# Adaptive max pooling: the loads of the first group walk each partition's run from its high end to its low end

## Chip, cores and metric

The kernel runs on one core of a Trainium2 chip. The metric is the device time of one execution in microseconds (us). Before the prediction, three runs of the kernel before gave 334.97 us (median; 334.90 to 335.02). The profile is one further execution, with a span of 333.2 us.

## The reference

```python
x = np.random.randn(32, 256, 4096).astype(np.float32)   # batch, channels, length
output_size = 256

for i in range(output_size):
    start = int(i * length / output_size)
    end = int((i + 1) * length / output_size)
    result[:, :, i] = np.max(x[:, :, start:end], axis=-1)
```

The length divides evenly, so each output is the maximum of 16 neighbouring values (64 B). 134.2 MB are read, 8.4 MB are written, and each value is used once.

## The kernel before

All outputs are one long list. It is split into group A (128 x 9340 outputs) and group B (128 x 7044), and inside a group each of the 128 partitions (the rows of the on-chip memory, SBUF) owns a contiguous run. The distance between the starts of two neighbouring partitions' runs is called the pitch: 597,760 B in group A, 450,816 B in group B. A load brings up to 1024 outputs' worth of every partition's run, 64 KiB per partition and 8.39 MB in all. VectorE, the compute engine that takes the maxima, reduces it in two pieces, and the outputs collect in the tile `kept`, which is stored at the end. In the code, `W` is the 16 values of one output.

```python
    CHUNK = 1024
    GAP = 152
    FIRST = 128
    LOADS_A, LOADS_B = 9, 6

    LESS = 4
    group_a = [FIRST] + [CHUNK] * (LOADS_A - 1) + [CHUNK - LESS]
    last = total - sum(group_a) - LOADS_B * CHUNK
    group_b = [CHUNK] * LOADS_B + [last]
    # ... cut ...
    for g, loads in enumerate((group_a, group_b)):
        xg, og = group(sum(loads))      # one contiguous run per partition
        a = 0
        for n in loads:
            xn = xg[:, a * W : (a + n) * W]
            dst = kept[:, base + a : base + a + n] if n != last else None
            if n == FIRST:
                # ... cut: the small first load and its reduction ...
            else:
                low = n_loads % 2 * (CHUNK + GAP)
                moved = n_loads // 2 % 2
                at = low + moved * GAP
                nc.sync.dma_start(out=ring[:, at * W : (at + n) * W], in_=xn)
                if n != last:
                    cut = CHUNK - GAP if moved else GAP
                    parts = [(0, cut), (cut, n)]
                    for u, v in parts if moved else parts[::-1]:
                        pooled(dst[:, u:v], at + u, v - u)
                # ... cut: the last load, reduced in place ...
                n_loads += 1
            a += n
        full = a - last if g else a
        stores.append((og[:, 0:full], kept[:, base : base + full]))
        base += full
```

The ring holds two loads and a gap. A new load goes over the larger part of the load before last, so it is issued as soon as that part's reduction (872 outputs) has ended, and does not wait for the smaller part (152). The two large stores are issued after the last load.

## Time and profile before

| | before |
|---|---|
| time, median of 3 | 334.97 us |
| VectorE busy | 276.5 us (83%) |
| 16 DMA engines busy with the queue of the loads and the two large stores | 98.8% |
| rate over the span | 428 GB/s |
| one full load, landing to landing | 19.3 to 19.4 us |
| VectorE's work for one full load | 17.28 us |

The lines behind these figures, and how they are read, are in the prediction. A landing is the moment when a load has arrived, read from the start of the reduction that waited for it; a round is the time from one landing to the next.

### The profile page before, as it was taken

How to read it: one execution, taken by the hardware profiler on the slowest of the kernel's cores; microseconds unless marked ns; L12 is line 12 of the kernel's file. 1: busy time of each engine (PE TensorE's matmuls, PEld its weight loads, DVE VectorE, ACT ScalarE, POOL GpSimd, SP SyncE). 2: the span in 40 equal slices, each digit the busy share in tenths (PEclk: the TensorE clock that was granted, in tenths of full speed). 3: DMA queues.
4: the chain of work that ended last, by engine and by line, in shares of the span. 5: the costliest groups of instructions: out<-in, count | busy, mean ns of one | idle time of the engine just before them, and what ended most of it. 6: DMA issues, size and time to landing. Idle time of an engine off the chain costs nothing.

```text
span 333.2 us, 113 instructions
## 1 busy us (share of the span) xinstructions
DVE 276.5 (83%) x32; POOL 0.2 (0%) x4
## 2 busy tenths in 40 slices
DVE  2009979797997979799797979979797998979993
POOL 0000000000000000000000000000000000000000
DMA  9898989899898989899898989899898989899987
GB/s 378 378 504 378 504 378 504 378 409 472 378 504 378 504 378 504 378 417 464 376 502 377 504 378 496 386 425 456 378 504 378 504 378 504 378 458 443 393 386 339
DMA packets 2880, 142.61 MB, mean 428 GB/s; under 512 B 320, under 2 KB 320, under 8 KB 448
## 3 DMA queue, kind: packets, MB, share of 16 engines
q1 hardware_dynamic: 2736, 142.15, 98.8%
q10 hardware_dynamic: 144, 0.46, 0.3%
HBM read 134.22 MB, written 8.39 MB: 428 GB/s over the span
## 4 chain that ended last, share of the span: by engine, by line
DMA 57%; DVE 36%; DVEq 5%; issue 0%; SPq 0%
DMA ring<-in_x_dram 57%; DVE kept L56 36%; DVEq L145 5%; SPq L85 0%
## 5 line engine op out<-in xcount | busy, mean ns | idle before, releaser
L56 DVE TENSOR_REDUCE kept<-ring 128x152 f32<-128x2432 f32 (+3 forms) x31 | 261.4, 8473 | 51.6 <-DMA ring<-in_x_dram 51.6
L56 DVE TENSOR_REDUCE ring<-ring 128x900 f32<-128x14400 f32 x1 | 15.1, 15141 | 0.0
L131 POOL MEMSET const-bfloat16-1.0<- 128x1 bf16 x1 | 0.1, 102 | 0.0
L131 POOL MEMSET const-uint8-127<- 128x1 uint8 x1 | 0.1, 101 | 0.0
L131 POOL MEMSET const-float32-0.0<- 128x1 f32 x1 | 0.1, 99 | 0.2 <-issue 0.2
L131 POOL MEMSET const-float32-1.0<- 128x1 f32 x1 | 0.1, 98 | 0.0
## 6 DMA issues: line engine op xcount, KB each, us to landing
ring<-in_x_dram SPq DMA_DIRECT2D x1, 8160.0 KB, 24.0
ring<-in_x_dram SPq DMA_DIRECT2D x1, 7200.0 KB, 21.6
out_dram<-kept SPq DMA_DIRECT2D x1, 4670.0 KB, 32.4
out_dram<-kept SPq DMA_DIRECT2D x1, 3072.0 KB, 18.1
ring<-in_x_dram SPq DMA_DIRECT2D x1, 1024.0 KB, 4.6
out_dram<-ring ACTq DMA_DIRECT2D x1, 450.0 KB, 4.2
ring<-in_x_dram SPq DMA_DIRECT2D x14, 24.0
```

The source lines that it names most:

```text
L56: nc.vector.reduce_max(out=dst, in_=ring[:, at * W : (at + n) * W].rearrange("p (n w) -> p n w", w=W), axis=mybir.AxisListType.X,)
L131: nc = _bacc.Bacc("TRN2", target_bir_lowering=False, num_devices=1)
L145: with _tile.TileContext(nc) as tc:
```

## The change

The ten loads of group A keep their sizes and their order in time, but the first one now takes the top of each partition's run, and the following ones walk down. The place in `kept` moves along, so the result and the stores stay. The intent was to learn whether the direction of the walk through memory is worth something.

```diff
--- before.py
+++ after.py
@@ -76,8 +76,10 @@
     base = 0
     for g, loads in enumerate((group_a, group_b)):
         xg, og = group(sum(loads))
-        a = 0
+        a = sum(loads) if g == 0 else 0
         for n in loads:
+            if g == 0:
+                a -= n
             xn = xg[:, a * W : (a + n) * W]
             dst = kept[:, base + a : base + a + n] if n != last else None
             if n == FIRST:
@@ -102,8 +104,9 @@
                     last_kept = ring[:, end - n : end]
                     pooled(last_kept, at, n)
                 n_loads += 1
-            a += n
-        full = a - last if g else a
+            if g:
+                a += n
+        full = a - last if g else sum(loads)
         stores.append((og[:, 0:full], kept[:, base : base + full]))
         base += full
     assert taken == total
```

## The prediction

> **What bounds the kernel now.** I read the page first, from the top: busy shares, the row of the DMA engines, and the bytes moved.
>
> ```profile
> span 333.2 us, 113 instructions
> ...
> DVE 276.5 (83%) x32; POOL 0.2 (0%) x4
> ...
> DMA  9898989899898989899898989899898989899987
> ...
> HBM read 134.22 MB, written 8.39 MB: 428 GB/s over the span
> ```
>
> One compute engine works at all, for 83% of the span; the 16 DMA engines are nearly full in every slice (the 8s and 9s come from the way a 64 KiB packet is booked to a slice). The mean of 428 GB/s is over everything, start and tail included. So the DMA engines are the suspect, and the next view must say whether they ever pause. That is the stretches view, cut at the landings of the loads; its last two columns are the DMA share and GB/s. Group A is the loads up to about 179 us, group B those from there to 312.8, and the last stretch is the stores.
>
> ```profile
> 0.00:24.73 24.73, 2.29 (x1) 0.20 (x4) 1.00 1.00 424
> 24.73:44.10 19.37, 17.28 (x2) 0.00 (x0) 1.00 1.00 433
> ...
> 121.50:140.90 19.40, 17.28 (x2) 0.00 (x0) 1.00 1.00 432
> 140.90:160.30 19.40, 17.28 (x2) 0.00 (x0) 1.00 1.00 432
> ...
> 218.30:237.70 19.40, 17.28 (x3) 0.00 (x0) 1.00 1.00 432
> ...
> 312.80:333.20 20.40, 15.29 (x2) 0.00 (x0) 1.00 0.89 382
> ```
>
> Every load of 8.39 MB takes 19.3 to 19.4 us, with the DMA share at 1.00, and VectorE needs only 17.28 us of that. The reader is to see two things: the DMA engines set the pace, not VectorE, and group A (24.73 to 160.30) and group B (218.30 to 237.70) run at the same rate.
>
> The third view is the chain that ended last. It looks as if VectorE and loads alternate:
>
> ```profile
> 24.75 14.70 DVE kept L56
> 39.45 0.02 issue
> 39.47 24.06 DMA ring<-in_x_dram
> 63.52 0.02 issue
> 63.55 14.70 DVE kept L56
> ```
>
> This is not a proof that VectorE is on the path. A load is issued at 39.47, when the 14.70 us reduction has freed its room, and lands at 63.52; but the load before it landed only at 44.13 (where the next reduction starts in the timeline). For 44.13 - 39.47 = 4.66 us the new load waits behind the previous one in a full queue. The remaining 19.4 us are its own transfer. So VectorE has about 4.7 us of room in each round before the queue would run dry, less the gap between last byte and semaphore. The view of waits agrees: VectorE waits for loads, and nobody else waits on the compute side.
>
> ```profile
> DVE kept L56 <- DMA ring<-in_x_dram: 51.6, 16, 17.1
> ```
>
> Of these 51.6 us, 17.1 is the first full load and 5.4 the small one before it; the other 14 waits are about 2.1 us each, which is 19.35 - 17.28.
>
> Last, the packet records of the trace: each partition's row is one packet of 65,536 bytes, its median time is 2.418 to 2.422 us in every full load, in group A and group B, and the worst of all is 2.64 us. 16 engines x 65,536 B / 2.418 us = 433.6 GB/s. A time that constant looks like a fixed limit of the engine or its port and not like memory that answers now well and now badly.
>
> **What the Trainium skill says.** "DMA: Bandwidth & Descriptors", section "Where 436 GB/s comes from", gives the ceiling on the SBUF side as 16 ports x 256 bits x 850 MHz = 435.2 GB/s. The trace agrees: 432 to 435 in the full stretches. "HBM Reference", section "Specifications (TRN2)", gives about 716 GB/s to the pair of cores that share a memory, and says that a core streaming alone is bounded by its 16 DMA engines. With one core running, the trace has 433, so by these pages some 280 GB/s of memory bandwidth are idle, an estimate from the two. The DMA page, section "Latency and other measured facts", reports that rows whose pitch is a large power of two (512 KiB and up) cost half the rate or more, and that padding by 4 KiB cures it. That is the one thing by which addresses alone could matter here. The same page, section "How a descriptor splits into AXI transactions", says that a run that does not start at a multiple of 256 B fetches bytes that it does not use. The trace of before shows neither loss.
>
> **The change part by part.** Only the source address and the place in `kept` move, and only for the ten loads of group A.
>
> - Removed or added: no instruction, no byte, no semaphore. The list of sizes is walked in the same order (128, then eight of 1024, then 1020), so the first load is still 1.0 MB, the ring slots alternate as before (they depend on the count of loads, not on the offset), and the reductions have the same 32 shapes. VectorE: 276.5 us before and after, difference 0.
> - Moved, source: one partition's run of group A is 9340 x 64 B = 597,760 B. Before, the loads start at 0, 8,192, 73,728 and so on upwards inside it; after, at 589,568, 524,032, ..., 65,280 and 0. The pitch between partitions stays 597,760 B = 2335 x 256, no power of two. The new starts are multiples of 256 as well (524,032 = 2047 x 256; 65,280 = 255 x 256). Modulo 4096, partition p of a full load started at -256p before and starts at -256(p + 1) now: the same set of 16 residues, shifted by one partition. Inside one row the bytes still go upwards, and the distance between the 16 rows in flight is unchanged. Cost: ten loads at an unchanged 433 GB/s, 0.
> - Moved, target: `kept` of group A is filled from the top. Start addresses of the reductions' outputs in it were multiples of 32 B and are now multiples of 16 B (1020 x 4 = 4080). VectorE reads 16 values for each one it writes, so I expect nothing; were a reduction a few hundred ns longer, it would vanish in the 2.1 us of idle time and the 4.7 us of queue.
> - The stores: same bytes, same shape, same order. All of group A's outputs are there when its last reduction ends near 197 us, and its store is issued at 291.5 us, after the last load. Cost 0.
>
> Sum: 0, so 334.97 stays, rounded to 335.0.
>
> **The rivals.** First, a memory rate that depends on the addresses: running backwards breaks a neighbourhood that the memory used. Before, the next load starts where the last ended, in the same partition's run, but some 19 us later, and after 8.4 MB of other addresses. For it: this kernel's odd size of 1020 suggests that somebody tuned the pitch. Against it: pitch and stagger are what that tunes, and they stay; and the kernel before holds a natural trial, since group B has another pitch (450,816 B, residues going up instead of down) and the same 432 GB/s. What it would make: 2% is 6.7 us, over about 175 us of group A's transfers a rate 3.8% lower, 417 instead of 433 GB/s. Five per cent lower would give about 344 us.
>
> Second, a new wait: the tracker of dependences could see the descending writes into `kept`, or the moved slice of 1020, as a hazard and hold a load or the first store. For it: the code that orders things looks at addresses. Against it: within a group no two reductions write the same part of `kept` and none reads it; the ring, where the real hazards are, is addressed exactly as before. If the first store were held until the last reduction, it would cost up to its own transfer, 4.78 MB at 433 = 11 us, of which part lies beside that reduction; some 340 us.
>
> Third, a gain. The loads could run nearer to the skill's 435.2 GB/s: at most 0.4% of 175 us, 0.7 us. The start cannot gain, since the first load is as small as before and VectorE then waits for the second one anyway. Over 2% faster has no room in a stretch that is full at 433.
>
> Fourth, the transfer that is hidden anyway: VectorE's changed alignment, above. Hidden in both directions.
>
> **Range and chances.** The three runs of before span 0.12 us, and the steps above sum to 0. The range must hold a different chip or run, and tenths of a microsecond from slow packets (the first full loads of before had a few of 2.5 to 2.6 us, about 0.1 us per load when spread over 16 engines). I take 334.4 to 335.8, a little longer upwards, as losing rate is possible and gaining it hardly is. Within 2%: 0.96. Slower by over 2%: 0.03, the first two rivals. Faster by over 2%: 0.01.
>
> **What would show it.** Right: the stretches between landings in group A stay at 19.3 to 19.4 us and 432 to 435 GB/s, packets stay near 2.42 us, VectorE's sum stays at 276.5 us, the first store is still issued near 291.5 us, and the chain has the same 36 pieces. Wrong by the first rival: group A's stretches over 20 us with DMA share 1.00 and fewer GB/s, group B's unchanged. Wrong by the second: a pause in the DMA row, or the first store issued after 310 us. Wrong on the target's alignment: a mean of the 872-wide reduction other than 14.69 us, with no effect on the span below some 16.7 us (14.69 + 2.07).

## The result and the profile after

The changed kernel took 334.92 us (median of 6 runs, 334.86 to 335.00), the kernel before 334.97 us (6 runs, 334.83 to 335.13). The ratio is 0.9999, with a 95% interval of 0.9986 to 1.0012. A ratio here is the mean time of one kernel's runs over that of the other's of the same rounds, so it is not quite the ratio of the medians. Executions over 1.5% slower than the fastest of the same kernel are left out of the means.

Set side by side, the two programs have the same instructions in the same order on every engine; only line numbers differ. The page of the kernel after:

```profile
span 333.1 us, 113 instructions
...
DVE 276.5 (83%) x32; POOL 0.2 (0%) x4
...
HBM read 134.22 MB, written 8.39 MB: 428 GB/s over the span
```

The span is 0.1 us shorter, and the other lines shown are as before. The stretches of the kernel after, over the same windows (length, VectorE busy, two columns without use here, DMA share, GB/s):

```profile
24.73:44.10 19.37, 17.28 (x2) 0.00 (x0) 1.00 1.00 433
121.50:140.90 19.40, 17.30 (x3) 0.00 (x0) 1.00 1.00 432
140.90:160.30 19.40, 17.32 (x3) 0.00 (x0) 1.00 1.00 432
...
218.30:237.70 19.40, 17.33 (x3) 0.00 (x0) 1.00 1.00 432
...
312.80:333.20 20.40, 15.16 (x2) 0.00 (x0) 1.00 0.89 382
```

The first three of these are group A, which now goes downwards; the rates are those of before to the last digit. The 17.30 to 17.33 in place of 17.28 come from where the windows cut: the reductions start some hundredths earlier. The groups of reductions by shape (busy us, mean ns of one, idle before), in the kernel before:

```profile
L56 DVE TENSOR_REDUCE kept<-ring 128x872 f32<-128x13952 f32 x14 | 205.6, 14686 | 44.3 <-DMA ring<-in_x_dram 44.3
L56 DVE TENSOR_REDUCE kept<-ring 128x152 f32<-128x2432 f32 x15 | 40.1, 2676 | 0.0
```

And after:

```profile
L56 DVE TENSOR_REDUCE kept<-ring 128x872 f32<-128x13952 f32 x14 | 205.6, 14686 | 44.1 <-DMA ring<-in_x_dram 44.1
L56 DVE TENSOR_REDUCE kept<-ring 128x152 f32<-128x2432 f32 x15 | 40.1, 2676 | 0.0
```

The means are the same to the nanosecond. So the moved target cost nothing either, and the null is not a sum of two effects that cancel: source and target are each unchanged. The wait of VectorE after, as one line:

```profile
DVE kept L56 <- DMA ring<-in_x_dram: 51.5, 16, 17.1
```

It was 51.6 before. The packet records of the trace say the same for the memory side: 64 KiB packets took a mean of 2.421 us after and 2.422 us before, with 4 of 1792 over 2.5 us after and 18 before.

### The profile page after: what moved, and what is told of

The parts are those of the page before. It is cut to its first block, busy times and chain, and to the rows that moved or that the text cites. A ratio compares the mean times of both kernels' runs of the same rounds, so it can differ in the third digit from the quotient of the medians.

```text
span 333.1 us, 113 instructions
## 1 busy us (share of the span) xinstructions
DVE 276.5 (83%) x32; POOL 0.2 (0%) x4
## 4 chain that ended last, share of the span: by engine, by line
DMA 57%; DVE 36%; DVEq 5%; issue 0%; SPq 0%
DMA ring<-in_x_dram 57%; DVE kept L56 36%; DVEq L148 5%; SPq L87 0%
```

## Experiments

The theory was: the loads run at a limit (2.418 us for a 64 KiB packet on each of 16 engines) that lies in front of the memory, so that the order of the addresses is not seen; and VectorE lies beside the loads. The main rival was: the memory does care where the loads go, and upward and downward happen to suit it equally. A second rival took the chain of the profile literally, with VectorE on the path. All kernels give correct results but that of e1. Each group of runs has its own runs of the kernel before on the same chip (medians 334.86, 334.97 and 335.14 us).

### e1: read the same place nine times

```diff
-            xn = xg[:, a * W : (a + n) * W]
+            if g == 0 and n != FIRST:
+                xn = xg[:, FIRST * W : (FIRST + n) * W]
+            else:
+                xn = xg[:, a * W : (a + n) * W]
```

The results of group A are wrong.

> Nine full loads of group A all read the first full load's 8.39 MB again (outputs of group A wrong on purpose; every instruction and byte count as before). Theory (the engine and port limit of 2.418 us per 64 KiB packet sets the pace, the memory's order is not seen): 335.0 us within 0.3%, packets at 2.42 us. Rival (the memory's neighbourhood matters, and the forward and the backward walk happen to be equally good or bad): rereading the same 8.39 MB must move the rate of group A, by more than 1% of the span in one direction or the other.

Measured: 335.50 us (335.33 to 335.91), ratio 1.0018 (1.0003 to 1.0033). The median packet is still 2.418 us, but 31 of 1792 took over 2.5 us, against 18 in the trace of before. In the middle of group A, the rate goes down a little and comes back in group B (the stretches of e1):

```profile
121.81:141.41 19.60, 17.28 (x2) 0.00 (x0) 1.00 0.99 428
141.41:160.99 19.58, 17.28 (x3) 0.00 (x0) 1.00 0.99 428
219.25:238.60 19.35, 17.27 (x3) 0.00 (x0) 1.00 1.00 434
```

Inside the 0.3% of the theory and far from the rival's 1%. Reading one place again and again gains nothing, and costs about 0.6 us (by the interval, 0.1 to 1.1 us). Why it costs those was not looked into.

### e2: shuffle both groups

```diff
-        for n in loads:
+        order = (0, 6, 1, 8, 4, 7, 2, 5, 3, 9) if g == 0 else (4, 1, 5, 0, 3, 2, 6)
+        starts = [sum(loads[:i]) for i in range(len(loads))]
+        for i in order:
+            a, n = starts[i], loads[i]
...
-            a += n
+            a = sum(loads)
```

> The loads of both groups in a scrambled order, with no two neighbours in a row in either direction; result correct. Theory: 335.0 us within 0.3%, stretches of 19.3 to 19.4 us. Rival (memory likes any regular walk, forward or backward): slower than 2%, rates under 425 GB/s in both groups.

Measured: 334.84 us (334.77 to 335.17), ratio 0.9998 (0.9983 to 1.0013). One pair of neighbours slipped through: in group B, load 2 follows load 3. Group A has none. A regular walk is worth nothing that 0.5 us would show in this layout. One stretch of group A and one of group B of e2:

```profile
121.54:140.89 19.35, 17.28 (x2) 0.00 (x0) 1.00 1.00 434
218.22:237.57 19.35, 17.28 (x3) 0.00 (x0) 1.00 1.00 434
```

### e3 and e4: a layout in which addresses cost something

A test that finds nothing must show that it could have found something. Here each partition's run is its whole 1 MiB of the input, so that the 16 rows in flight lie multiples of 1,048,576 B apart, not of 597,760 or 450,816 B. Sizes and instructions are as before. The rows of the stores move too: they now lie 65,536 B apart in the output, not 37,360 or 28,176 B. e3 walks up; e4 has the change on top.

```diff
-        span = slice(taken * P, (taken + n) * P)
+        lo = taken
         taken += n
         return (
-            xw[span].rearrange("(p n) w -> p (n w)", p=P),
-            ow[span].rearrange("(p n) -> p n", p=P),
+            xw.rearrange("(p n) w -> p (n w)", p=P)[:, lo * W : taken * W],
+            ow.rearrange("(p n) -> p n", p=P)[:, lo:taken],
         )
```

> Positive control: before's order, but one partition's run is its whole 1 MiB, so the pitch of the rows in flight is 1,048,576 B and no longer 597,760 or 450,816 B; same instructions and bytes, correct result. If addresses can be felt at all in this kernel, here: by the Trainium skill's pitch figures for 512 KiB to 4 MiB I estimate loads at 200 to 350 GB/s, so 420 to 700 us. If it is 335 us too, the memory's addresses are not felt even in the worst layout that I know, and the theory is stronger than I stated it.

> The same 1 MiB pitch with the changed kernel's downward order of the first group. Theory: order is not seen even where the memory may be the limit, so the same as e3 within 1%. Rival (order matters once the memory is the bound, and it was hidden before only by the port limit): over 2% away from e3.

Measured: e3 353.53 us (352.78 to 355.84), ratio 1.0577 (1.0538 to 1.0616); e4 355.46 us (354.16 to 357.10), ratio 1.0614 (1.0578 to 1.0650). So addresses can be felt in this kernel, which is what the control was for. The stores have little part in it: of the 17.8 us by which the profiled span of e3 is longer (351.0 us for 333.2), 16.2 have come by the issue of the first large store (307.70 us for 291.50). My estimate of 420 to 700 us was far too high, and the fault is in how I read the page, in the prediction too. The Trainium skill ("DMA: Bandwidth & Descriptors", section "Latency and other measured facts") has 207 GB/s at a pitch of 512 KiB, 164 at 2 MiB and 103 at 4 MiB, where a padded pitch has 214. The loss is about half at 4 MiB; at 512 KiB it is 3%, and at 2 MiB 23%. The 5.5 to 5.8% by which the kernel got longer here at 1 MiB lie between these. The stretches of e3, cut at its landings:

```profile
28.61:51.59 22.98, 17.28 (x3) 0.00 (x0) 1.00 0.99 385
91.03:111.33 20.30, 17.28 (x2) 0.00 (x0) 1.00 0.99 423
111.33:131.05 19.72, 17.28 (x2) 0.00 (x0) 1.00 0.99 415
131.05:151.70 20.65, 17.28 (x2) 0.00 (x0) 1.00 0.99 413
```

This is what the first rival would have looked like in the changed kernel: the DMA share stays at 0.99 while the GB/s go down, VectorE's 17.28 us do not move, and the rounds are uneven. In the packet records, 487 of the 1792 packets took over 2.5 us, while the fastest still took 2.415 us: the floor stays, and packets are held up above it.

The two intervals overlap, so the question of order was still open here.

### e5: without the stagger between partitions

```diff
-    LESS = 4
+    LESS = 0
```

> Four more outputs per partition in group A: pitch 598,016 B = 146 x 4096 instead of 597,760 B, so all rows of a load start at the same place modulo 4096 (the stagger of 256 B from partition to partition is gone), in before's upward order. Theory (pitch and stagger are what addresses can matter by): same as before within 0.3% if the stagger is without need, or slower in group A alone; packets tell. No theory has order in it here; it tells whether the stagger that the change keeps is what keeps it free.

Measured: 334.64 us (334.54 to 334.73), ratio 0.9990 (0.9973 to 1.0006). The pitch of group A is now a multiple of 4096 B, all its rows start alike, and it costs nothing. The edit does the same to group B, whose pitch becomes 450,560 B = 110 x 4096 (its last load shrinks to 896 outputs). The stagger, on which my prediction leant ("the same set of 16 residues"), isn't what keeps the change free.

### e6: odd starts

```diff
-    FIRST = 128
+    FIRST = 129
...
-    LESS = 4
+    LESS = 5
```

> First load 129 wide, the ninth full one 1019: every later load of group A starts at a multiple of 64 B that is not one of 256 B, and the outputs in kept start at multiples of 4 B that are not multiples of 16; pitch as before, result correct. Theory: 335.0 us within 0.3%, reductions of 872 still 14.69 us; by the skill's account of unaligned starts at most one extra read of 256 B in 64 KiB, 0.4% of group A's 175 us = 0.7 us. Rival (alignment of source or target is felt, and the change was free only since it kept multiples of 256 B and 16 B): over 1% slower, or longer reductions.

Measured: 335.06 us (334.88 to 335.17), ratio 1.0003 (0.9988 to 1.0018). The 872-wide reductions took 14.687 us. Starts that are no multiples of 256 B (source) or 16 B (target) aren't felt at this resolution, some 0.5 us. The estimate of 0.7 us, worked out from the Trainium skill ("DMA: Bandwidth & Descriptors", section "How a descriptor splits into AXI transactions": a row that starts off 256 B fetches from the 256 B boundary below its start), is at the edge of it, so this run neither shows nor excludes it.

### e7 and e8: more work for VectorE

In the full rounds of group A, some outputs of the smaller piece are computed again. e7 has `extra, width = 1, 76`, e8 has `2, 148`.

```diff
                         pooled(dst[:, u:v], at + u, v - u)
+                    if g == 0:
+                        u = cut if moved else 0
+                        for _ in range(extra):
+                            pooled(dst[:, u : u + width], at + u, width)
```

> In each of the nine full rounds of group A, VectorE does 76 outputs once more (about 1.4 us, from 2.676 us for 152 and 14.686 for 872: 16.7 ns per output). VectorE then needs 18.7 of 19.35 us. Theory (VectorE lies beside the loads, 2.07 us of idle time per round): 335.0 us within 0.3%, idle before the large reductions down from 2.07 to about 0.65 us. Rival (the chain that ended last is to be taken literally, reduction then load then reduction): up to 9 x 1.4 = 12.7 us slower.

> The same with 2 x 148 outputs once more, about 5.2 us per round: VectorE needs 22.5 us against 19.35 for a load. Theory: the bound moves to VectorE in group A; followed round by round from the timeline of before (a load costs about 2 us more than its transfer when the queue has run dry, from the first load's landing of 4.6 us for 2.4 us of transfer) I estimate 25 us more, about 360 us, range 354 to 364. If VectorE had more room than thought, under 350.

Measured, e7: 335.04 us (335.01 to 335.16), ratio 1.0003 (0.9988 to 1.0018). The added 12.8 us of VectorE work are gone in its idle time (timelines: start, length, what, and in brackets the idle time before it). One line of the kernel before:

```profile
82.88 17.28 DVE L56 TENSOR_REDUCE kept<-ring 128x872 f32<-128x13952 f32 x2 [2.05 <-DMA ring<-in_x_dram]
```

Two of e7:

```profile
63.50 18.73 DVE L56 TENSOR_REDUCE kept<-ring 128x872 f32<-128x13952 f32 x3 [0.61 <-DMA ring<-in_x_dram]
82.85 18.73 DVE L56 TENSOR_REDUCE kept<-ring 128x872 f32<-128x13952 f32 x3 [0.62 <-DMA ring<-in_x_dram]
```

The reductions start 19.35 us apart, as before, and the gap before them is 0.61 or 0.62 us in place of about 2.07. The literal reading of the chain, which wanted up to 12.7 us, is refuted.

Measured, e8: 362.41 us (362.23 to 362.48), ratio 1.0819 (1.0803 to 1.0835). Now VectorE sets the pace of group A. The chain that ended last, e8 (start, length, what):

```profile
157.25 19.82 DVE kept L56 x3
177.06 0.02 issue
177.09 2.63 DVE kept L56
179.72 0.02 issue
179.74 19.82 DVE kept L56 x3
...
224.66 17.22 DVE kept L56 x2
241.88 0.02 issue
241.90 22.05 DMA ring<-in_x_dram
```

A round is 179.74 - 157.25 = 22.49 us, and from the landing of the first full load to 241.90 no load stands in the chain; in the kernel before, every second round had one. This is the contrast by which to read such a chain: where VectorE really is the bound, as here, the loads drop out of it. The time is 2 us above the estimate of 360 and within its range. Part of that can be read off: the load at 241.90 took 22.05 us to land, 0.7 more than the 21.4 that I had reckoned. Its queue had run dry, and in e8 nine loads began after such a pause: of their 144 first packets (one on each of 16 engines), 136 took over 2.7 us and the longest 3.8, in place of 2.42. In the trace of before, none is over 2.7 us.

### e9, e10 and e11: direction in the costly layout, with more runs

e9 and e10 are e3 and e4 once more. e11 lets both groups go downwards:

```diff
-        for n in loads:
+        order = (0, 9, 8, 7, 6, 5, 4, 3, 2, 1) if g == 0 else (5, 4, 3, 2, 1, 0, 6)
+        starts = [sum(loads[:i]) for i in range(len(loads))]
+        for i in order:
+            a, n = starts[i], loads[i]
...
-            a += n
+            a = sum(loads)
```

> e3 again, with more rounds, since e3 and e4 differed by half a per cent with runs that spread by as much. Upward order at a pitch of 1 MiB: 353 to 355 us.

> e4 again. Theory (order is not seen even where addresses cost time): within 0.5% of e9, intervals that overlap. Rival (downward is worse once the memory is felt): 0.5% or more above e9, like 355.5 against 353.9 before, with intervals apart.

> Pitch of 1 MiB with the loads of both groups downward (the last, smaller load of each list keeps the place that its part of the code needs: 1020 first in group A, 900 last in group B). Theory: within 0.5% of e9. Rival: about 15 loads instead of 9 go downward, so 15/9 of what e10 loses against e9, about 0.8%.

| pitch of 1 MiB | median (range), us | runs | ratio to before (95%) |
|---|---|---|---|
| e9, upward | 353.78 (352.01 to 355.43) | 6 | 1.0545 (1.0517 to 1.0573) |
| e10, group A downward | 356.30 (354.70 to 357.59) | 5 | 1.0632 (1.0610 to 1.0653) |
| e11, both downward | 355.10 (354.63 to 355.68) | 4 | 1.0597 (1.0584 to 1.0611) |

Here my theory in its strict form is wrong. With e3 and e4 taken in, the mean is 353.8 us over 10 upward runs and 355.9 us over 9 with group A downward, 0.6% apart, the same sign both times, and the intervals of e9 and e10 do not overlap. Single runs do: upward they lie between 352.0 and 355.8 us, downward between 354.2 and 357.6. So where addresses cost time, the kernels of the two orders differ, by about 2 us in 354. But it isn't a price per downward load: e11 sends more loads downward and lost less (1.0597 / 1.0545 is 0.5% above e9, where the rival's dose wanted 15/9 of e10's 0.8%, so 1.4%; the 0.8% on record was reckoned from e3 and e4). The landings do not locate it: the last load of group A landed at 192.16 and 194.42 us in the two profiles of upward, and at 194.47 and 194.10 us in the two of downward, so one profile of the same kernel differs from the next by as much as is looked for.

The packet records point to group A, in two profiles of each order. Of the 1152 packets of its nine large loads, 355 and 365 took over 2.5 us upward (e3, e9), and 468 and 493 with group A downward (e4, e10). In group B, whose order is the same in all four, it is 188 and 145 against 182 and 199 of 768. The mean packet of group A is 2.553 us upward and 2.583 downward; over the 72 packets of each engine that is an estimate of 2.2 us, the size that is looked for.

Direction is not the only thing that differs there. At this pitch every row of a load starts at the same place modulo 4096 B. In e3 and e9 the full loads of group A start at a multiple of 4096 B. In e4 and e10 the 1020-wide load lies at the bottom of the run, so the others start 256 B below such a multiple. e11 goes down with starts at the multiples, and there some 332 packets of group A took over 2.5 us, no more than upward. So by this one profile going down is not enough to make the slow packets, though e11 as a whole took 0.5% more than e9. The shifted starts may be what makes them, but no run walks up with such starts. What makes the 2 us stays open.

No run points to a version that beats both kernels: e5's 0.1% has an interval that includes 1.

## Why the prediction was right

- **The sum of zero.** 335.0 us was predicted, 334.92 measured, in a range of 334.4 to 335.8. Each term held by itself: no instruction changed, group A's rate stayed at 432 to 433 GB/s, the reductions stayed at 14.686 and 2.676 us, and the first large store was issued at 291.37 us (before 291.50).
- **The loads' limit hides the order.** Shown for this layout by e2, where a scrambled order costs the same. e1 adds that not even a stay in one place speeds the loads up. That the limit is the engine or its port, and not some rate of the memory that no layout here changes, is only argued: no packet of 64 KiB in any trace was faster than 2.415 us, and 16 of them in that time are 434.2 GB/s, next to the 435.2 that the Trainium skill ("DMA: Bandwidth & Descriptors", section "Where 436 GB/s comes from") gives for the SBUF ports.
- **VectorE beside the loads.** Shown by e7 and e8: 1.4 us more per round vanish, 5.2 us more do not. One reading in the prediction is too generous, though: "about 4.7 us of room in each round" is how late a single round may be. Lateness of every round adds up, and then the room is the idle time of 2.07 us: in e8, 5.24 us more work made the round 22.49 - 19.35 = 3.14 us longer, where 4.7 us of room would have left about 0.5. The prediction's sum did not use it.
- **The first rival** asked the right question. Its mechanism exists, by e3 and e9 with their 5.5 to 5.8%, but needs another pitch, and even there the changed order, with the starts that it shifts, is worth 0.6%.
- **A page misread, and reasons that were not needed.** The prediction had it from a page of the Trainium skill that every pitch of a large power of two from 512 KiB up costs half the rate or more, and took this for the only way in which addresses could matter. The page doesn't say that (its figures are under e3); it was one of the two losses of which the prediction says that the trace shows neither. It did no harm, since the pitch stays. Residues modulo 4096 and starts at multiples of 256 B were part of the argument; e5 and e6 broke them, without a loss. The result was right, but these two supports carried nothing. That two groups with different pitches ran equally fast in the kernel before was the better evidence.
- **What the stretches' 8s and 9s mean** was explained in passing by the booking of packets. The packet records bear it out: when each packet's time is spread over the slices that it covers, the share is 1.00 in all 38 inner slices. One stretch was not as the prediction has it ("DMA share at 1.00" for every load): the last full load's, 276.40 to 295.70 us, has 0.99 and 428 GB/s, before and after.

## What to carry to other kernels

Where the loads' queue never ran dry and nearly every packet took the same time, as here, the order in which equal loads were issued gained and cost nothing. Look for that in the packet rate of two parts of the kernel with different layouts, before any edit; an order can also move the start addresses, so check those too. A chain that alternates between reduction and load does not say that both bound the kernel: subtract the time that a load waits behind its predecessor, or add a little work and see whether it vanishes. And give a null result a control that can fail: here it was a pitch of 1 MiB, which cost 19 us at the same bytes and instructions.

## What the Trainium skill lacked or had wrong

- "DMA: Bandwidth & Descriptors", section "Latency and other measured facts": its figures on the pitch of rows are from copies inside the memory in rows of 16 KiB, with none for 1 MiB and none for loads to SBUF. Here loads in rows of 64 KiB at a pitch of 1 MiB made the kernel 5.5 to 5.8% longer (353.5 and 353.8 us for 334.9 and 335.1, e3 and e9), which fits between the page's 512 KiB and 2 MiB.
- The same page, section "How a descriptor splits into AXI transactions": starts off 256 B cost nothing that 0.5 us would show in 64 KiB rows (e6, ratio 1.0003). The page gives no measured price for long rows.
- No page that I read says how much longer the first packets of a load from SyncE take when its queue had run dry: in e8, 136 of 144 such packets, of 64 KiB or just under, took over 2.7 us, up to 3.8, against 2.42 in a full queue.
- No page that I read says whether the order of large loads matters: not in these layouts (e2, ratio 0.9998), and by 0.6% at a pitch of 1 MiB (e3, e4, e9 and e10), where the start addresses shift with the order and the cause stays open.
